# Staging the transposed weights of a stick-breaking attention in SBUF before they are split into two halves

## The chip, the cores and the metric

The kernel runs on one core of one Trainium2 chip. The core's engines work side by side and are ordered among themselves by semaphores alone: TensorE (PE; its weight loads are listed as PEld), VectorE (DVE), ScalarE (ACT), GpSimd (POOL) and SyncE (SP), which issues the DMAs here. The metric is the device time of one execution in microseconds. The kernel before takes 1668.99 us, the median of three runs (1668.65 to 1670.77).

## The reference

One layer of a streaming encoder: 1024 frames of a new stream and 32 frames of a running one, D_MODEL 1024. A combined projection feeds a retention group (4 heads) and a stick-breaking group (8 heads of 64); their outputs are projected and normalised, then come an attention into 256 memory tokens and a gated feed-forward part with a causal convolution. The change lies in the stick-breaking attention:

```python
def stick_breaking_block(q, k, v, q_pos, k_pos):
    """q (B,H,Tq,d); k,v (B,H,Tk,d). A[t,s] = beta[t,s] prod_{s<j<t}(1-beta[t,j]), s<t."""
    z = jnp.einsum('bhqd,bhkd->bhqk', q, k).astype(jnp.float32) * (SB_DH ** -0.5)
    valid = k_pos[None, :] < q_pos[:, None]
    log_fail = jnp.where(valid, jax.nn.log_sigmoid(-z), 0.0)
    after = lax.cumsum(log_fail, axis=3, reverse=True) - log_fail
    a = jnp.where(valid, jnp.exp(jax.nn.log_sigmoid(z) + after), 0.0)
    return jnp.einsum('bhqk,bhkd->bhqd', a, v.astype(jnp.float32)).astype(v.dtype)
```

All of it is fp32.

## The kernel before

Matmuls of full precision are made of faster ones: every operand is kept as two halves in the matmul type fp32r, `hi` and `lo`, with `lo = raw - hi`, and a product is `hi*hi + hi*lo + lo*hi`. The helper `split` makes the halves: ScalarE copies `raw` into `hi` with a cast (line 103), then VectorE writes `raw - hi` into `lo` (line 104). `mm` (line 119) issues a matmul.

The stages follow one another: first query/key projections and the values; a woven stage, in which the rest of the projections and the retention group run together with the stick-breaking group; the end of retention; the output projection; the memory attention; its projection; the feed-forward part.

In the woven stage the function `weave` (line 125) takes two lists of steps with costs, `main` (projections and retention tiles) and `side` (stick-breaking), and calls them in one order, so that both use up their costs at the same rate. That is the order of the code. The builder of the program then fixes the order of the instructions on each engine when it compiles, from the dependencies and its own estimates, so that neighbours in the code may change places; at run time each engine keeps its order.

A stick-breaking head works on blocks of 128 queries, i = 0 to 7, with 128*(i+1) keys:

- `score(i)` (line 421): TensorE makes scores in PSUM banks of tag "pb" (two buffers). ScalarE makes of each bank `f = sigmoid(-z/8)` (line 434) and `b = sigmoid(z/8)` (line 435), two SBUF tiles of 128x1024 with two buffers each. POOL puts 1 and 0 above the diagonal (lines 437, 439). VectorE makes of `f` the running product from the right, in place (the scan, line 441), and multiplies `b` by it, shifted by one (line 443). `b` then holds the weights, and `f` isn't read any more.
- `turn(i, g)` (line 446): TensorE transposes up to four 128x128 tiles of `b` into one PSUM bank of tag "pc" (line 457), and `split` makes the halves `ah` and `al` (tag "at", listed as `ath` and `atl`) from that bank.
- `value(i)` (line 463), for odd i: TensorE multiplies values by the halves of two blocks, into a bank of tag "pd" (listed as `pv`).

`stick_steps` (line 566) strings these together: score(i+1) comes before the turns of block i, and the values of a pair one block later still. `stick_sample` (line 483) does the same for the running stream, once for two heads.

The tag "pc" has two banks, and they are shared: retention's `turn` (lines 302 and 303, copied out by ScalarE in line 305) and `store` (line 341, copied out in line 343) take turns with the stick-breaking transposes. A bank can be written again when the readers of its last contents are done; for a stick-breaking bank these are ScalarE's cast and VectorE's subtraction. In the same way a buffer of `f` can be written again when the last reader of its former contents is done.

Other names in the trace: `acc` are the banks of projections, `rps` those of retention; `ra` and `rb` are retention's rotated queries and keys, `sg` its gate, `ss` its sum of squares, of which POOL makes the power -1/2 (lines 115 and 116) and by which ScalarE scales (line 337).

Of the kernel before, what the change touches and what calls it, by code (L numbers as in the profile page):

```python
# [18 lines left out]
NS = 32  # L19
# [47 lines left out]
def trunk(ctx: ExitStack, tc: tile.TileContext, I, O):  # L67
    nc = tc.nc
# [30 lines left out]
    def raw_tile(shape, name):  # L99
        return rawp.tile(shape, F32, name=name, tag="raw")  # L100

    def split(raw, hi, lo):
        nc.scalar.copy(hi, raw)  # L103
        nc.vector.tensor_tensor(out=lo, in0=raw, in1=hi.bitcast(F32), op=ALU.subtract)  # L104
# [13 lines left out]
    def mm(out, lhsT, rhs, start, stop):  # L118
        nc.tensor.matmul(out, lhsT, rhs, start=start, stop=stop)  # L119
# [56 lines left out]
    def tr_tile():  # L176
        return bank("pc", "tr")
# [203 lines left out]
    def z_tile():  # L381
        return bank("pb", "z")

    def pv_tile():
        return bank("pd", "pv")

    def fold_o(pv, e, w):
# [4 lines left out]
        nc.vector.tensor_tensor(out=ot[sl, :w], in0=pv[0:64, :w], in1=ot[sl, :w], op=ALU.add)  # L392
        return ot[sl, :w]

    def dup_load(raw, src):
        dma(out=raw[0:64], in_=src)
        dma(out=raw[64:128], in_=src)

    def stick_head(hd):
        m, e = hd // 2, hd % 2  # L400
        rows = slice(64 * hd, 64 * hd + 64)
        H, F, AT = {}, {}, {}

        def prepare():
            qr = raw_tile([128, NP], f"qr{hd}")
            dup_load(qr, qT_s[rows, 0:NP])
            kr = raw_tile([128, NP], f"kr{hd}")
            dup_load(kr, O["kT"][rows, 0:NP])
            vr = raw_tile([128, 8, 64], f"vr{hd}")
            dma(out=vr, in_=O["v"][0:NP, rows].rearrange("(t p) d -> p t d", p=128))  # L410
            q = sb.tile([128, NP], F32R, name="sq_", tag="sbq", bufs=2)
            nc.scalar.copy(q, qr)
            nc.vector.tensor_tensor(out=q[64:128], in0=qr[64:128], in1=q[64:128].bitcast(F32), op=ALU.subtract)
            kh = sb.tile([128, 1088], F32R, name="kh", tag="kst", bufs=3)
            kl = sb.tile([128, 1088], F32R, name="kl", tag="kst", bufs=3)
            split(kr, kh[:, :NP], kl[:, :NP])
            v = sb.tile([128, 10, 128], F32R, name="v", tag="sbv", bufs=2)
            split(vr, v[:, 0:8, 0:64], v[:, 0:8, 64:128])
            H.update(q=q, kh=kh, kl=kl, v=v)

        def score(i):
            q, kh, kl = H["q"], H["kh"], H["kl"]
            w = 128 * (i + 1)
            npc = (w + 511) // 512
            pw = max(w // npc, 256)
            f = sb.tile([128, NP], F32, name="f", tag="f", bufs=2)
            b = sb.tile([128, NP], F32, name="b", tag="b", bufs=2)
            for pc in range(npc - 1, -1, -1):
                z = z_tile()
                c0 = pc * pw  # L430
                c1 = min(c0 + pw, w)
                mm(z[:, :pw], q[:, 128 * i:128 * i + 128], kh[:, c0:c0 + pw], True, False)
                mm(z[:, :pw], q[:, 128 * i:128 * i + 128], kl[:, c0:c0 + pw], False, True)
                nc.scalar.activation(f[:, c0:c1], z[:, :c1 - c0], AF.Sigmoid, scale=-0.125)
                nc.scalar.activation(b[:, c0:c1], z[:, :c1 - c0], AF.Sigmoid, scale=0.125)
            dg = slice(128 * i, w)
            nc.gpsimd.affine_select(out=f[:, dg], in_=f[:, dg], pattern=[[-1, 128]], compare_op=ALU.is_gt,  # L437
                                    fill=1.0, base=0, channel_multiplier=1)
            nc.gpsimd.affine_select(out=b[:, dg], in_=b[:, dg], pattern=[[-1, 128]], compare_op=ALU.is_gt,
                                    fill=0.0, base=0, channel_multiplier=1)  # L440
            nc.vector.tensor_tensor_scan(out=f[:, :w][:, ::-1], data0=f[:, :w][:, ::-1], data1=f[:, :w][:, ::-1],  # L441
                                         initial=1.0, op0=ALU.mult, op1=ALU.bypass)
            nc.vector.tensor_tensor(out=b[:, :w - 1], in0=b[:, :w - 1], in1=f[:, 1:w], op=ALU.mult)
            F[i] = b

        def turn(i, g):
            half = i % 2
            if half == 0 and g == 0:
                for gg in range((i + 5) // 4):
                    AT[gg] = tuple(sb.tile([128, 4, 256], F32R, name=x, tag="at", bufs=4) for x in ("ath", "atl"))  # L450
                jz = i + 1
                for x in AT[jz // 4]:
                    nc.gpsimd.memset(x[:, jz % 4, 0:128].bitcast(F32), 0.0)
            j0, j1 = 4 * g, min(4 * g + 4, i + 1)
            tr = tr_tile()
            for j in range(j0, j1):
                nc.tensor.transpose(tr[:, 128 * (j - j0):128 * (j - j0) + 128], F[i][:, 128 * j:128 * j + 128], ident)
            src = tr[:, :128 * (j1 - j0)].rearrange("p (a b) -> p a b", b=128)
            ah, al = AT[g]
            dsl = slice(128 * half, 128 * half + 128)  # L460
            split(src, ah[:, 0:j1 - j0, dsl], al[:, 0:j1 - j0, dsl])

        def value(i):
            pv = pv_tile()
            for j in range(i + 1):
                ah, al = AT[j // 4]
                mm(pv[:, :256], H["v"][:, j], ah[:, j % 4], j == 0, False)
                mm(pv[:, :256], H["v"][:, j], al[:, j % 4], False, j == i)
            o = fold_o(pv, e, 256)
            dma_out(out=mix_s[i - 1:i + 1, 64 * e:64 * e + 64, 4 + m].rearrange("t p c -> p t c"),  # L470
                    in_=o.rearrange("p (t c) -> p t c", t=2))

        blocks = []
        for i in range(8):
            tv = [(0.7 * min(4, i + 1 - 4 * g), lambda i=i, g=g: turn(i, g)) for g in range((i + 4) // 4)]
            if i % 2:
                tv.append((0.25 * (i + 1), lambda i=i: value(i)))
            blocks.append(((0.6 * (i + 1), lambda i=i: score(i)), tv))
        return (2.0, prepare), blocks
# [3 lines left out]
    def stick_sample(m):  # L483
        H = {}
# [27 lines left out]
        def score():  # L512
            q, kh, kl = H["q"], H["kh"], H["kl"]
            f = sb.tile([128, NP], F32, name="f", tag="f", bufs=2)
            b = sb.tile([128, NP], F32, name="b", tag="b", bufs=2)
            for c0, cw in ((0, PAST), (PAST, NS)):
                z = z_tile()
                for e in range(2):
                    mm(z[:64, :cw], q[:, e], kh[:, e, c0:c0 + cw], e == 0, False)
                    mm(z[:64, :cw], q[:, e], kl[:, e, c0:c0 + cw], False, e == 1)  # L520
                nc.scalar.activation(f[:64, c0:c0 + cw], z[:64, :cw], AF.Sigmoid, scale=-0.125)
                nc.scalar.activation(b[:64, c0:c0 + cw], z[:64, :cw], AF.Sigmoid, scale=0.125)
            nc.vector.tensor_tensor(out=f[:64, PAST:NK], in0=f[:64, PAST:NK], in1=cst[:64, C_INV:C_INV + 32], op=ALU.max)
            nc.gpsimd.tensor_tensor(out=b[:64, PAST:NK], in0=b[:64, PAST:NK], in1=cst[:64, C_VAL:C_VAL + 32], op=ALU.mult)
            nc.vector.tensor_tensor_scan(out=f[:64, :NK][:, ::-1], data0=f[:64, :NK][:, ::-1], data1=f[:64, :NK][:, ::-1],
                                         initial=1.0, op0=ALU.mult, op1=ALU.bypass)
            nc.vector.tensor_tensor(out=b[:64, :NK - 1], in0=b[:64, :NK - 1], in1=f[:64, 1:NK], op=ALU.mult)
            H["b"] = b

        def turn():  # L530
            b = H["b"]
            tr = tr_tile()
            ah = sb.tile([128, 5, 64], F32R, name="ath", tag="at", bufs=4)
            al = sb.tile([128, 5, 64], F32R, name="atl", tag="at", bufs=4)
            for j in range(5):
                cw = 128 if j < 4 else NS
                nc.tensor.transpose(tr[:cw, 64 * j:64 * j + 64], b[:64, 128 * j:128 * j + cw], ident[:64, :64])
            split(tr[:, 0:256].rearrange("p (a b) -> p a b", b=64), ah[:, 0:4], al[:, 0:4])
            split(tr[:NS, 256:320], ah[:NS, 4], al[:NS, 4])
            H.update(ah=ah, al=al)  # L540

        def value():
# [14 lines left out]
        def store():  # L557
# [4 lines left out]
            dma_out(out=mixs_s[:, 4 + m], in_=ot[:, :NS])  # L562

        return (2.0, prepare), [((2.5, score), [(1.5, turn), (1.5, value), (0.3, store)])]

    def stick_steps():
# [914 lines left out]
    for t in range(4):  # L1481
        for j in range(LATE):
            i = len(STEPS) - LATE + j
# [99 lines left out]
```

## Time and profile before

| | |
|---|---|
| median of three runs | 1668.99 us |
| the profiled execution, its own time | 1672.11 us |
| its span, first to last instruction | 1670.4 us |
| granted TensorE clock, mean | 0.993 |
| HBM read, written | 163.75 MB, 42.36 MB |
| woven stage, as used here | 103 to 502 us of the span |

Lines of the profile read so. A row of instructions in order of time has its start and its duration in us, the engine, the line of the code, the operation, the tile written and the tiles read, the shape, and in brackets the engine's idle time before it with what ended that. A row of a group has the count, then the busy time in us and the mean duration in ns, then the idle time before these instructions and what ended most of it. A row of waits has the waiting engine and tile, what it waited for, and the sum in us, the number and the longest. A row of a window has the busy time of PE, PEld, DVE, ACT and POOL in it, each with its number of instructions, and the granted clock, the share of DMA and GB/s. Of the forty slices each digit is a share of busy time in tenths. The ends of matmuls are modelled.

### The profile page before, as it was taken

How to read it: one execution, taken by the hardware profiler on the slowest of the kernel's cores; microseconds unless marked ns; L12 is line 12 of the kernel's file. 1: busy time of each engine (PE TensorE's matmuls, PEld its weight loads, DVE VectorE, ACT ScalarE, POOL GpSimd, SP SyncE). 2: the span in 40 equal slices, each digit the busy share in tenths (PEclk: the TensorE clock that was granted, in tenths of full speed). 3: DMA queues.
4: the chain of work that ended last, by engine and by line, in shares of the span. 5: the costliest groups of instructions: out<-in, count | busy, mean ns of one | idle time of the engine just before them, and what ended most of it. 6: DMA issues, size and time to landing. Idle time of an engine off the chain costs nothing. (4 is left out here: it accounts for less than half of the span.)

```text
span 1670.4 us, 26878 instructions
## 1 busy us (share of the span) xinstructions
PE 1618.0 (97%) x10008; PEld 1448.5 (87%) x10008; DVE 1192.0 (71%) x1912; ACT 795.6 (48%) x1588; POOL 293.2 (18%) x616
## 2 busy tenths in 40 slices
PE   8999999989999999999999989999999999999997
PEld 8889787877777879999977879999999999888885
DVE  3147879788775575655555798777777777689968
ACT  4246556565645122543523255554555455444445
POOL 0012246453444110000001101000010000002004
PEclk9999999999999999999999989999999999999999
DMA  7244304123214443532363313232233322498942
GB/s 257 84 118 139 83 26 104 56 72 85 57 51 150 136 139 125 158 123 82 107 200 117 117 42 114 102 98 93 102 102 101 101 91 101 139 352 275 318 160 101
DMA packets 108547, 207.87 MB, mean 124 GB/s; under 512 B 23328, under 2 KB 48672, under 8 KB 108416
## 3 DMA queue, kind: packets, MB, share of 16 engines
q1 hardware_dynamic: 108416, 206.15, 38.4%
q8 instruction: 78, 1.28, 0.3%
q14 instruction: 53, 0.43, 0.1%
HBM read 163.75 MB, written 42.36 MB: 123 GB/s over the span
## 5 line engine op out<-in xcount | busy, mean ns | idle before, releaser
L1031 PE MATMUL ux<-op_s,w_t 128*128 128x266 f32 x1056 | 140.6, 288 | 1.3 <-DVE op_s L104 1.3
L1151 DVE SCALAR_TENSOR_TENSOR cv<-u,cw,cv 128x1058 f32<-128x1058 f32 x88 | 116.0, 1319 | 33.0 <-ACT cv L1149 32.9
L1031 PEld LDWEIGHTS ux<-op_s,w_t 128*128 128x128 f32 x1056 | 135.2, 191 | 2.5 <-DVE op_s L104 2.4
L1339 PE MATMUL dx<-wdo 128*128 128x512 f32 x528 | 124.3, 392 | 0.0
L1339 PEld LDWEIGHTS dx<-wdo 128*128 128x128 f32 x528 | 100.2, 190 | 21.0 <-issue 0.2
L441 DVE TENSOR_TENSOR_SCAN f<-f 128x128 f32<-128x128 f32 (+3 forms) x64 | 88.9, 1388 | 30.0 <-POOL f L437 14.0
L115 POOL TENSOR_SCALAR rs<-mv 128x1 f32<-128x1 f32 (+1 forms) x27 | 36.6, 1355 | 357.6 <-ACT junk L638 192.2
L1339 PE MATMUL dy<-wdo 128*128 128x512 f32 x396 | 93.2, 389 | 0.1
L1339 PEld LDWEIGHTS dy<-wdo 128*128 128x128 f32 x396 | 74.3, 188 | 16.0 <-DVE wdo L104 0.5
L103 ACT CAST w_t<-wup 128x512 fp32r<-128x512 f32 x88 | 54.0, 618 | 58.2 <-PE ux L1031 44.5
L104 DVE TENSOR_TENSOR w_t<-wup,w_t 128x512 fp32r<-128x512 f32 x88 | 60.4, 688 | 29.6 <-ACT w_t L103 29.6
L119 PE MATMUL acc<-wo,mh 128*128 128x512 f32 x256 | 80.3, 393 | 0.0
L1031 PE MATMUL uy<-op_s,w_t 128*128 128x266 f32 x528 | 72.0, 291 | 3.5 <-ACT op_s L103 2.5
L1031 PEld LDWEIGHTS uy<-op_s,w_t 128*128 128x128 f32 x528 | 68.8, 193 | 4.5 <-ACT op_s L103 2.9
L1031 PEld LDWEIGHTS uy<-op_x,w_w 128*128 128x128 f32 x504 | 67.8, 196 | 4.6 <-DVE u L1179 1.8
L1031 PE MATMUL uy<-op_s,w_w 128*128 128x266 f32 x528 | 70.1, 287 | 0.9 <-DVE op_s L104 0.9
L1149 ACT ACTIVATE cv<-u,cw 128x1058 f32<-128x1058 f32 x44 | 56.1, 1274 | 30.0 <-POOL u L1143 29.0
L1031 PE MATMUL uy<-op_x,w_w 128*128 128x266 f32 x504 | 68.7, 294 | 1.6 <-DVE u L1179 1.6
L1031 PE MATMUL ux<-op_x,w_t 128*128 128x266 f32 x528 | 69.3, 287 | 0.0
L1031 PE MATMUL ux<-op_x,w_w 128*128 128x266 f32 x528 | 68.8, 286 | 0.0
L1031 PEld LDWEIGHTS uy<-op_s,w_w 128*128 128x128 f32 x528 | 67.0, 189 | 1.8 <-DVE op_s L104 1.8
L1031 PEld LDWEIGHTS ux<-op_x,w_t 128*128 128x128 f32 x528 | 67.2, 190 | 0.1
(519 smaller groups left out, 4428.9 us busy)
## 6 DMA issues: line engine op xcount, KB each, us to landing
wup<-in_wup SPq DMA_DIRECT2D x44, 512.0 KB, 3.5
rdq<-hid_s SPq DMA_DIRECT2D x85, 256.0 KB, 5.3
rdq<-in_wdown SPq DMA_DIRECT2D x74, 256.0 KB, 5.4
wds<-in_wdown SPq DMA_DIRECT2D x22, 512.0 KB, 3.5
hid_s<-cv SPq DMA_DIRECT2D x22, 512.0 KB, 2.6
rwr<-in_wret SPq DMA_DIRECT2D x16, 512.0 KB, 3.6
x_s<-r SPq DMA_DIRECT2D x16, 512.0 KB, 2.6
qr<-qT_s SPq DMA_DIRECT2D x16, 256.0 KB, 4.0
```

Source lines behind the costliest of these rows:

```text
L103: nc.scalar.copy(hi, raw)
L104: nc.vector.tensor_tensor(out=lo, in0=raw, in1=hi.bitcast(F32), op=ALU.subtract)
L115: nc.gpsimd.tensor_scalar(out=out, in0=var, scalar1=eps, scalar2=None, op0=ALU.add)
L119: nc.tensor.matmul(out, lhsT, rhs, start=start, stop=stop)
L441: nc.vector.tensor_tensor_scan(out=f[:, :w][:, ::-1], data0=f[:, :w][:, ::-1], data1=f[:, :w][:, ::-1], initial=1.0, op0=ALU.mult, op1=ALU ...
L1031: nc.tensor.matmul(acc[:, j, :266], W[:, p, k], X[:, k, q, c], start=start and k == 0 and n == 0, stop=stop and k == 3 and n == 2, skip_gr ...
L1149: nc.scalar.activation(cv, u[:, 2:UW], AF.Identity, scale=cw[:, f, 2:3], bias=cw[:, f, 3:4])
L1151: nc.vector.scalar_tensor_tensor(out=cv, in0=u[:, j:UW - 2 + j], scalar=cw[:, f, j:j + 1], in1=cv, op0=ALU.mult, op1=ALU.add)
L1339: nc.tensor.matmul(acc, x[:, a, ts_], w[:, b], start=start and n == 0, stop=stop and n == 2, skip_group_check=True)
```

## The change

A new helper, `split_staged`, has ScalarE copy the PSUM bank to an SBUF tile as it is, and then calls `split` on that tile. In `turn`, the tile is the part of `f` that belongs to the same columns. So for every bank there is one ScalarE copy more; the cast and the subtraction read SBUF, and the bank's only reader is the copy. The readers of `f` are now, last of all, the subtractions. The sample's `turn` is changed likewise, with two copies for its two pieces. There are 104 splits of this kind: 96 in the heads and 8 in the samples.

```diff
+    def split_staged(tr, stage, hi, lo):
+
+        nc.scalar.copy(stage, tr)
+        split(stage, hi, lo)
+
...
-        H, F, AT = {}, {}, {}
+        H, F, FS, AT = {}, {}, {}, {}
...
             F[i] = b
+            FS[i] = f
...
             src = tr[:, :128 * (j1 - j0)].rearrange("p (a b) -> p a b", b=128)
+            stage = FS[i][:, 128 * j0:128 * j1].rearrange("p (a b) -> p a b", b=128)
             ah, al = AT[g]
             dsl = slice(128 * half, 128 * half + 128)
-            split(src, ah[:, 0:j1 - j0, dsl], al[:, 0:j1 - j0, dsl])
+            split_staged(src, stage, ah[:, 0:j1 - j0, dsl], al[:, 0:j1 - j0, dsl])
...
-            H["b"] = b
+            H.update(f=f, b=b)
...
-            split(tr[:, 0:256].rearrange("p (a b) -> p a b", b=64), ah[:, 0:4], al[:, 0:4])
-            split(tr[:NS, 256:320], ah[:NS, 4], al[:NS, 4])
+            stage = H["f"][:, 0:320]
+            split_staged(tr[:, 0:256].rearrange("p (a b) -> p a b", b=64),
+                         stage[:, 0:256].rearrange("p (a b) -> p a b", b=64), ah[:, 0:4], al[:, 0:4])
+            split_staged(tr[:NS, 256:320], stage[:NS, 256:320], ah[:NS, 4], al[:NS, 4])
```

## The prediction

> **What bounds the kernel now.** I read the page first: the shares of the engines and the forty slices.
>
> ```profile
> PE 1618.0 (97%) x10008; PEld 1448.5 (87%) x10008; DVE 1192.0 (71%) x1912; ACT 795.6 (48%) x1588; POOL 293.2 (18%) x616
> PE   8999999989999999999999989999999999999997
> DVE  3147879788775575655555798777777777689968
> ACT  4246556565645122543523255554555455444445
> ```
>
> TensorE (PE) is busy from end to end; whatever doesn't change a wait of PE changes nothing. The edited lines run where stick-breaking is woven with the projections and retention, 103 to 502 us (slices 3 to 12, where VectorE is busiest too). So next the busy times of that stretch (PE, PEld, DVE, ACT, POOL, then clock and DMA), its groups of instructions by shape, and two rows of the page for the same pair of operations with SBUF sources:
>
> ```profile
> 103.00:502.00 399.00, 380.70 (x2227) 320.17 (x2226) 319.24 (x591) 241.70 (x639) 164.39 (x340) 1.00 0.29 80
> ```
> ```profile
> L103 ACT CAST ath<-tr 128x512 fp32r<-128x512 f32 x48 | 28.2, 591 | 12.6 <-PE tr L457 11.0
> L104 DVE TENSOR_TENSOR atl<-tr,ath 128x512 fp32r<-128x512 f32 x48 | 32.7, 680 | 4.2 <-ACT ath L103 4.1
> L103 ACT CAST ath<-tr 128x384 fp32r<-128x384 f32 x16 | 7.7, 481 | 1.4 <-PE tr L457 1.2
> L103 ACT CAST ath<-tr 128x256 fp32r<-128x256 f32 x20 | 7.5, 376 | 5.0 <-PE tr L457 3.4 <-PE tr L537 1.2
> L103 ACT CAST ath<-tr 128x128 fp32r<-128x128 f32 x16 | 4.3, 269 | 3.2 <-PE tr L457 2.8
> L337 ACT ACTIVATE sg<-sg,ss 128x128 f32<-128x128 f32 x25 | 10.1, 402 | 32.2 <-POOL ss L116 29.3 <-DVE ot L392 2.1 <-DVE sg L324 0.7
> ```
> ```profile
> L103 ACT CAST w_t<-wup 128x512 fp32r<-128x512 f32 x88 | 54.0, 618 | 58.2 <-PE ux L1031 44.5
> L104 DVE TENSOR_TENSOR w_t<-wup,w_t 128x512 fp32r<-128x512 f32 x88 | 60.4, 688 | 29.6 <-ACT w_t L103 29.6
> ```
>
> PE is idle 399.0 - 380.7 = 18.3 us of this stretch, VectorE 80, ScalarE 157. The clock is full (1.00) and DMA at 0.29. The view of waits says who ends PE's idle time (us, times, longest); the rows that matter, four for PE and three for its weight loads:
>
> ```profile
> PE tr L341 <- DVE atl L104: 4.5, 5, 2.0
> PE tr L457 <- DVE atl L104: 3.3, 4, 1.4
> PE tr L302 <- DVE atl L104: 1.5, 2, 1.3
> PE tr L457 <- ACT qk L305: 1.0, 1, 1.0
> PEld tr L341 <- DVE atl L104: 6.2, 6, 2.4
> PEld tr L457 <- DVE atl L104: 4.9, 6, 1.8
> PEld pv L119 <- DVE atl L104: 2.7, 6, 0.9
> ```
>
> The first three are one thing: a transpose wants one of the two "pc" banks, and the bank still waits for VectorE's subtraction. That is 4.5 + 3.3 + 1.5 = 9.3 us in 11 waits, half of PE's idle time here. The longest of them, in order of time:
>
> ```profile
> 367.40 0.40 PE L119 MATMUL acc<-wr_0h,x 128*128 128x512 f32 x1
> 367.74 0.58 ACT L103 CAST ath<-tr 128x512 fp32r<-128x512 f32 x1
> 369.07 0.68 DVE L104 TENSOR_TENSOR atl<-tr,ath 128x512 fp32r<-128x512 f32 x1
> 369.81 0.33 PE L341 MATMUL tr<-ident,sg 128*128 128x128 f32 x1 [2.01 <-DVE atl L104]
> ```
>
> ScalarE had read the bank by 368.32, VectorE by 369.75, and PE went on 0.06 us later.
>
> **Term 1, the banks.** After the change a bank is free when ScalarE's plain copy ends, which takes the place of the cast in the queue. Here PE would wait from 367.80 to about 368.38, so 0.58 of its 2.01 us stays. Allowing some 0.4 us for each of two more such remainders, I take 9.3 - 1.3 = 8.0 us off PE. The bounds are 0 (PE only meets VectorE at the next buffer) and 6.2 + 4.9 = 11.1 us, the same stalls as the weight loads show them, whose ends aren't modelled.
>
> **Term 2, ScalarE's work.** The copies have the shapes of the casts: 48 x 591 + 16 x 481 + 20 x 376 + 16 x 269 ns = 47.9 us, and four 32-row ones of 0.2 us each. The casts now read SBUF, for which the nearest row says 618 instead of 591: 48 x 27 ns = 1.3 us. ScalarE goes from 241.7 to about 292 of 399 us, 73%; its 157 us of idle time hide that, and it costs only where someone waits for the pair. The subtractions keep their length (680 with a PSUM operand, 688 from SBUF), so VectorE's sum stays at 319. [...]
>
> **Term 3, the values' matmuls.** `value` reads the halves, and these come one copy later. That is on PE's path where PE starts within a copy of the subtraction's end. I compared the 32 groups of `value` in the heads with the last subtraction that each needs: in 12 the slack is shorter than the copy's length. The first and the last of the 12:
>
> ```profile
> 111.07 0.42 DVE L104 TENSOR_TENSOR atl<-tr,ath 128x256 fp32r<-128x256 f32 x1
> 111.72 0.28 PE L119 MATMUL pv<-atl,v 128*128 128x256 f32 x1
> 494.41 0.69 DVE L104 TENSOR_TENSOR atl<-tr,ath 128x512 fp32r<-128x512 f32 x1 [1.38 <-ACT ath L103]
> 495.16 0.39 PE L119 MATMUL pv<-atl,v 128*128 128x256 f32 x1
> ```
>
> In the first the slack is 111.72 - 111.49 = 0.23 against a copy of 0.38, in the last 0.06 against 0.59. Each lacks its copy (and 0.06 for the hand-over) less its slack; over the 12 that is 4.5 us on PE. Bounds: 0, if the copies are placed earlier than the casts were, and 12 x 0.65 = 7.8 us.
>
> **Term 4, a new wait on ScalarE.** The copy goes into `f`, the scan's tile, of which there are two. So the first sigmoid of block i+1, which writes the same buffer, must wait for the last subtraction of block i-1; until now it waited only for VectorE's product, long done. Of the 66 blocks that have such a predecessor, 37 now start that sigmoid before that subtraction ends, the first and the last of them being:
>
> ```profile
> 108.12 0.53 ACT L434 ACTIVATE f<-z 128x384 f32<-128x384 f32 x1
> 108.92 0.26 DVE L104 TENSOR_TENSOR atl<-tr,ath 128x128 fp32r<-128x128 f32 x1
> 488.26 0.55 DVE L104 TENSOR_TENSOR atl<-tr,ath 128x384 fp32r<-128x384 f32 x1
> 488.50 0.60 ACT L521 ACTIVATE f<-z 64x512 f32<-64x512 f32 x1
> ```
>
> They overlap by 1.06 and 0.31 us; all 37 sum to 52 us of ScalarE standing still, if its order stays. Behind the waiting sigmoid stand the sigmoids of `b` that free the "pb" banks, the copies of `qk` and `ro` that free "pc" banks, and retention's evacuations; POOL's selects and VectorE's scan wait for the sigmoids, PE for the `qk` copy and the banks. How much reaches PE? The nearest row is another stall at the head of ScalarE's queue: at L337 it stands 29.3 us for POOL, and PE's waits behind ScalarE's `qk` copies are 1.0 us, 3%. Doubling that, since ScalarE is now fuller, gives 6% of 52 = 3.0 us. Bounds: 0, if other work is ordered ahead of the sigmoid, and a quarter, 13 us.
>
> **The sum.** -8.0 + 4.5 + 3.0 = -0.5 us. The profiled execution takes 1672.11 us (span 1670.4), 3.1 above the median of the three runs; it would take 1671.6, and the median of 1668.99 becomes 1668.5. About 0.2%, 3.3 us, is what a measurement can tell from no change here, so this forecast is "the same".
>
> **The rivals.**
>
> Faster: the banks' gain stays whole and the costs are hidden. For it speaks that the 11 waits are real idle time of the bounding engine, and that ScalarE and VectorE have 157 and 80 us of idle time to absorb lateness; against it, that a third of the `value` groups have no slack. Terms 3 and 4 at their lower ends give -8.0, 1661.0 us, and 1657.9 with term 1 at -11.1.
>
> Slower, by term 4: ScalarE's queue is held by VectorE's backlog and so becomes the carrier of the lateness that the banks carried. Place: the first sigmoid of a block. Price: at a quarter of 52 us, -8.0 + 4.5 + 13 = +9.5, 1678.5 us. It decides once more than 13% of the 52 us reaches PE (then the sum passes +3.3). For it speaks that the waiting engine is in front of both PSUM banks and POOL's chain; against it the 3% above, and that the order of instructions on an engine isn't the code's and may move the sigmoid back.
>
> Slower, by VectorE and POOL getting into each other's way. POOL's power of `ss` takes 0.57 us alone but 1.97 beside a scan, and a subtraction with two SBUF operands took 0.69 us once and 0.85 while POOL worked:
>
> ```profile
> 364.77 1.75 DVE L441 TENSOR_TENSOR_SCAN f<-f 128x768 f32<-128x768 f32 x1
> 364.91 1.97 POOL L116 TENSOR_TENSOR ss<-ss,mhalf 128x1 f32<-128x1 f32 x1
> 376.34 0.57 POOL L116 TENSOR_TENSOR ss<-ss,mhalf 128x1 f32<-128x1 f32 x1
> 400.03 0.69 DVE L104 TENSOR_TENSOR v<-vr,v 128x512 fp32r<-128x512 f32 x1 [1.71 <-ACT v L103]
> 404.18 0.85 DVE L104 TENSOR_TENSOR v<-vr,v 128x512 fp32r<-128x512 f32 x1
> ```
>
> The 104 edited subtractions read one operand from PSUM now and both from SBUF afterwards. At 0.16 us each they would cost VectorE 16.6 us; with half of it on PE's path the sum is -0.5 + 8.3 = +7.8, 1676.8 us. Against it: VectorE is 80% busy, not full, and most POOL work is short. [...]
>
> The change doesn't free the bank: if the second bank's copy had to wait for the first bank's subtraction, since both use one tile `f`, term 1 would be nothing and the sum +7.5, 1676.5 us. Against it: POOL's select on the last columns of an `f` starts before ScalarE's sigmoid of the other columns of that `f` ends, so parts of a tile are kept apart:
>
> ```profile
> 369.73 0.29 POOL L437 TENSOR_SCALAR_AFFINE_SELECT f<-f 128x128 f32<-128x128 f32 x1 [2.85 <-ACT f L434]
> 369.96 0.57 ACT L434 ACTIVATE f<-z 128x448 f32<-128x448 f32 x1
> ```
>
> **How the numbers follow.** The same: 0.36, at 1668.5, by itself 1665.7 to 1672.3. Faster: 0.34, around 1661. Slower: 0.20 by ScalarE's wait, 0.08 by the ports, 0.02 by banks that stay held, 0.30 in all. The likeliest case holds little over a third, so the range has to reach far into both others: from 1658, the far end of the fast case (about 0.08 lies below), to 1681, beyond the three slow ones (about 0.1 lies above, where more than a quarter of the sigmoids' wait counts).
>
> **What would show it.** In the changed profile, between 103 and 502 us: the rows of PE's `tr` waiting for DVE `atl` are gone, those waiting for ScalarE's copy are below 1.5 us; 104 copies more on ScalarE, its busy time near 292 us; the wait of `pv` for `atl` rises from 2.7 towards 7 us; a new row "ACT f L434 <- DVE atl" of some tens of us; the subtraction of 512 columns within 10 ns of 680, if the ports are no matter. PE's idle time stays near 18 us. The prediction is wrong if the weave ends more than 3.3 us earlier or later with these rows as said (then a share was mis-sized), or if the order of instructions on the engines has become so different that PE's waits come from elsewhere.

## The result and the profile after

The changed kernel takes 1687.91 us (median of four runs, 1687.01 to 1689.41) against 1668.82 us of the kernel before: 19 us more, a ratio of 1.0112 with a 95% interval of 1.0100 to 1.0124. The forecast was no change, 1658 to 1681 us. It is slower than the range allowed.

In the changed code the sigmoids stand in lines 439 and 440, POOL's selects in 442 and 444, the scan in 446, the product in 448, the transposes in 463, and the new copy in 397. The page's row of engines and two of its slices:

```profile
PE 1622.9 (96%) x10008; PEld 1444.6 (86%) x10008; DVE 1196.6 (71%) x1912; ACT 838.8 (50%) x1692; POOL 303.0 (18%) x616
PE   8999998999999999999999979999999999999997
ACT  4247667676665212533541356554555445444445
```

TensorE's busy time has hardly moved (1618.0 to 1622.9); ScalarE has 104 instructions and 43 us more. The windows say where the time is. The woven stage, which took 103 to 502 us, now ends at 521.5. Busy times of PE, PEld, DVE, ACT and POOL in it and in the two stretches behind it, first after and then before:

```profile
103.00:521.50 418.50, 389.56 (x2227) 320.99 (x2226) 323.96 (x591) 284.77 (x743) 173.44 (x340) 1.00 0.28 77
521.50:970.00 448.50, 443.24 (x2595) 393.23 (x2595) 272.21 (x510) 160.92 (x345) 55.11 (x71) 1.00 0.41 131
970.00:1685.00 715.00, 693.31 (x4698) 644.09 (x4696) 576.11 (x785) 361.47 (x556) 72.81 (x195) 0.99 0.42 142
```
```profile
502.00:951.00 449.00, 443.73 (x2599) 393.78 (x2599) 272.61 (x509) 160.84 (x345) 55.57 (x71) 1.00 0.41 132
951.00:1670.00 719.00, 697.15 (x4694) 648.76 (x4692) 575.88 (x785) 361.42 (x555) 71.68 (x195) 0.98 0.42 141
```

The woven stage is 19.5 us longer, the next stretch the same, and the last one 4 us shorter at a clock of 0.99 instead of 0.98. That last difference belongs to these two executions; it is why the spans differ by 14.9 us and the medians by 19.

So 2227 matmuls take 19.5 us longer in this stage. These rows of PE's waits matter now (us, times, longest), with the weight loads' two longest, the new waits of ScalarE, and two of VectorE that have grown:

```profile
PE rps L119 <- DVE sm L312: 7.3, 10, 1.4
PE pv L119 <- DVE atl L104: 7.0, 14, 0.9
PE tr L302 <- POOL ra L297: 4.0, 3, 2.3
PE pv L119 <- ACT ath L103: 1.8, 4, 0.9
PE tr L463 <- ACT f L397: 1.3, 1, 1.3
PE tr L341 <- ACT f L397: 0.7, 1, 0.7
```
```profile
PEld rps L119 <- DVE sm L312: 12.0, 12, 1.8
PEld pv L119 <- DVE atl L104: 12.0, 17, 1.3
```
```profile
ACT f L439 <- DVE atl L104: 27.3, 32, 1.9
ACT f L528 <- DVE atl L104: 2.2, 2, 2.0
```
```profile
DVE f L446 <- POOL f L442: 28.2, 34, 1.8
DVE atl L104 <- ACT ath L103: 18.5, 21, 1.7
```

In the kernel before, the corresponding rows of 103 to 502 us were:

```profile
PE rps L119 <- DVE sm L312: 1.8, 4, 0.6
PE pv L119 <- DVE atl L104: 1.1, 2, 0.6
PE tr L302 <- POOL ra L297: 0.7, 1, 0.7
DVE f L441 <- POOL f L437: 14.0, 22, 1.6
DVE atl L104 <- ACT ath L103: 11.9, 19, 1.4
```

The edit did what it says: no transpose waits for VectorE's subtraction any more, where PE had stood 9.3 us, and the waits for the copy are 2.0 us. But PE now stands for other things: the values' matmuls (`pv`) wait for their halves, retention (`rps`) for VectorE's mask product `sm`, and retention's transposes for POOL's sum `ra`; the change touches neither `sm` nor `ra`. ScalarE's new wait at the block's first sigmoid is there, 29.5 us in 34 waits, and VectorE's scan waits for POOL's select 28.2 instead of 14.0 us. In the stage PE's idle time is 418.5 - 389.6 = 28.9 us where the prediction wanted it to stay near 18.

Since the modelled ends hide part of a stall, I counted PE's stalls another way for all kernels below: the time from one matmul's start to the next, beyond the median for that shape in the whole execution, where it is over 0.04 us, from 103 us to the last `pv` matmul. The rest of that stretch comes to 353 to 356 us in every kernel; the stalls make the difference. Beside them stands the lag: from the start of the last of a bank's transposes, plus 0.11 us, to the end of VectorE's subtraction for that bank, as a mean over the 96 banks of the heads. Stalls and lag are of the profiled execution; the medians and the ratios below are of fast executions, and three slow ones of over 4000 us (two of the kernel with the copy behind the cast, one of the kernel before) are left out.

| kernel | median us | PE's stalls us | at `tr` | at `pv` | at `rps` | lag us |
|---|---|---|---|---|---|---|
| before | 1668.8 | 43.7 | 18.7 | 4.1 | 5.2 | 2.79 |
| the change | 1687.9 | 63.0 | 15.6 | 16.8 | 13.1 | 3.95 |
| staged in the low half | 1680.8 | 57.8 | 20.9 | 10.8 | 10.3 | 3.58 |
| copy alone | 1681.1 | 55.7 | 26.2 | 5.1 | 6.3 | 3.17 |
| wait alone | 1683.4 | 55.8 | 23.1 | 6.3 | 7.6 | 3.28 |
| its control | 1670.5 | 45.5 | 18.5 | 3.8 | 6.6 | 2.80 |
| copy behind the cast | 1670.7 | 46.6 | 18.5 | 3.5 | 7.8 | 2.82 |
| high half first | 1683.3 | 57.9 | 25.8 | 5.8 | 10.8 | 3.26 |
| staged in `b` | 1684.1 | 59.0 | 20.5 | 10.3 | 12.5 | 3.70 |
| a third staged | 1674.0 | 49.8 | 19.1 | 5.5 | 8.5 | 3.33 |
| copy and wait, late bank | 1690.9 | 64.4 | 29.5 | 9.8 | 6.4 | 3.58 |
| three buffers of `f` | 1683.8 | 58.0 | 15.6 | 10.4 | 14.2 | 3.49 |
| its control | 1671.7 | 44.8 | 20.1 | 3.4 | 4.5 | 2.79 |
| no subtraction, staged | 1670.0 | 46.9 | 11.9 | 3.3 | 15.8 | - |
| no subtraction, not staged | 1664.0 | 38.5 | 9.8 | 2.5 | 11.6 | - |
| low halves last, not staged | 1667.7 | 42.0 | 16.1 | 3.2 | 6.1 | 2.72 |
| low halves last, staged | 1687.6 | 62.1 | 15.6 | 15.9 | 13.9 | 3.98 |

### The profile page after: what moved, and what is told of

It is laid out like the page before. It is cut to its first block, busy times and chain, and to the rows that moved or that the text cites. A ratio compares the mean times of both kernels' runs of the same rounds, so it can differ in the third digit from the quotient of the medians.

```text
span 1685.3 us, 26981 instructions
## 1 busy us (share of the span) xinstructions
PE 1622.9 (96%) x10008; PEld 1444.6 (86%) x10008; DVE 1196.6 (71%) x1912; ACT 838.8 (50%) x1692; POOL 303.0 (18%) x616
## 5 line engine op out<-in xcount | busy, mean ns | idle before, releaser
L446 DVE TENSOR_TENSOR_SCAN f<-f 128x128 f32<-128x128 f32 (+3 forms) x64 | 89.7, 1401 | 47.3 <-POOL f L442 28.2
L1348 PEld LDWEIGHTS dy<-wdo 128*128 128x128 f32 x396 | 74.2, 188 | 16.4 <-DVE wdo L104 1.1
L104 DVE TENSOR_TENSOR atl<-f,ath 128x512 fp32r<-128x512 f32 (+3 forms) x104 | 55.7, 546 | 19.0 <-ACT ath L103 18.5
```

The lines of the kernel that those rows point to most:

```text
L1348: nc.tensor.matmul(acc, x[:, a, ts_], w[:, b], start=start and n == 0, stop=stop and n == 2, skip_group_check=True)
```

## The experiments

The theories: (A) the wait of the first sigmoid on the last subtraction, since both use `f`, makes the 19 us; (B) the halves come later by a copy, and whoever reads them waits.

**Staged elsewhere, the copy alone, the wait alone.** The first kernel takes `f` out of the change:

```diff
-        nc.scalar.copy(stage, tr)
-        split(stage, hi, lo)
+        nc.scalar.copy(lo, tr)
+        split(lo.bitcast(F32), hi, lo)
```

> The change with another stage: the copy goes into the tile of the low halves, so f is free after VectorE's product as before the change, and everything else of the change stays (one copy more per bank, the bank free after the copy, cast and subtraction from SBUF). The copy rounds, so the low halves come out as zero and the weights lose their low part. Theory A, the first sigmoid's wait on f makes the 19 us: the time falls back to 1662 to 1672, the row of ACT f waiting for DVE atl is gone and PE's waits of rps for sm are near 5 us again. Theory B, the halves come one copy later and the values' matmuls wait for them: 1680 to 1688, and the waits of pv stay at 15 us.

Measured: 1680.8 us, ratio 1.0060 (1.0044 to 1.0076). The second kernel has the same copy, but splits the bank:

```diff
         nc.scalar.copy(lo, tr)
-        split(lo.bitcast(F32), hi, lo)
+        split(tr, hi, lo)
```

> The kernel before with the same copy ahead of each split, into the tile of the low halves, and the split still made from the PSUM bank: ScalarE's work and the later halves, without the earlier bank and without the wait on f. Theory A: little more than the banks' wait being longer by a copy, 1672 to 1678. Theory B: as slow as the change or slower, 1684 to 1694, with pv waiting 15 us or more.

Measured: 1681.1 us, 1.0064 (1.0046 to 1.0082). The third and the fourth are the kernel before with this line more, behind the split of a block's last bank; the control writes `scr`, a column of its own, in place of `FS[i][:, 0:1]`:

```diff
+            if j1 == i + 1:
+                c = al[:, 0, 128 * half:128 * half + 1].bitcast(F32)
+                nc.vector.tensor_tensor(out=FS[i][:, 0:1], in0=c, in1=c, op=ALU.add)
```

> The kernel before with the wait alone: behind the last subtraction of each block of a head VectorE adds two copies of a column of the low half into a column of f that nobody reads, so that the next block's first sigmoid in that buffer waits for the subtraction. 64 VectorE instructions more. Theory A: 10 to 19 us over its control, which writes elsewhere. Theory B: within 3 us of its control.

> Control: the same 64 small VectorE additions, written to a column of their own, so no wait on f. Both theories: 1669 to 1675, the price of 64 small instructions on an engine that is 80% busy.

Measured: 1683.4 us (1.0076, 1.0060 to 1.0092) with the wait and 1670.5 us (1.0007, 0.9998 to 1.0017) without. Both theories hold, each for a part: the wait alone costs 12.9 us over its control by the medians and 11.5 by the ratios, the copy alone 12 and 11. And the first two kernels are equal, although the first frees the bank after the copy and the second only after the subtraction. PE's waits show how. In the copy-only kernel the banks are held longer and PE stands for them:

```profile
PE tr L341 <- DVE atl L104: 6.5, 6, 2.3
PE tr L462 <- DVE atl L104: 5.1, 3, 2.5
PE tr L302 <- DVE atl L104: 4.7, 5, 2.1
PE rps L119 <- DVE sm L312: 1.9, 5, 0.7
PE pv L119 <- DVE atl L104: 1.0, 3, 0.5
```

In the staged one these three rows are gone; the stalls at `tr` are 20.9 instead of 26.2 us, but those at `pv` 10.8 instead of 5.1 and at `rps` 10.3 instead of 6.3. What the early bank gave, PE lost elsewhere. The two kernels differ in one thing more, though: the staged one's casts and subtractions read SBUF. In it retention's transposes stand for POOL's `ra`, in the copy-only one not at all:

```profile
PE tr L302 <- POOL ra L297: 6.1, 4, 2.7
```

So the equal times show what the early bank is worth together with the SBUF operands, not by itself.

In the wait-only kernel, ScalarE's row is the one that the change has too, with VectorE's new addition as the releaser:

```profile
ACT f L435 <- DVE f L466: 25.7, 22, 2.4
```

**Work or lateness.** Is the copy's cost ScalarE's 48 us of work, or that it stands ahead of the cast? The first kernel here is the kernel before with one copy behind each split, from the high half into used columns of `b` (the samples likewise); the second casts from the bank first and copies then.

```diff
             split(src, ah[:, 0:j1 - j0, dsl], al[:, 0:j1 - j0, dsl])
+            nc.scalar.copy(F[i][:, 128 * j0:128 * j1].rearrange("p (a b) -> p a b", b=128), ah[:, 0:j1 - j0, dsl].bitcast(F32))
```

> The kernel before, with a ScalarE copy of the same size behind each split that nobody waits for: the high halves are copied into the columns of b that the transposes have read, and the next writer of that buffer is ScalarE itself. ScalarE has the 48 us of work, but the cast comes first and the halves aren't later by a copy of their own. Theory B1, the halves' lateness makes the 11.7 us that the copy alone cost: 1669 to 1674, and VectorE's waits of atl for ath near 12 us as before. Theory B2, ScalarE's extra work as such, by whatever stands behind it in its queue: 1678 to 1684.

> The copy into the low halves' tile once more (low halves zero), but the cast reads the bank and comes first, then the copy, then the subtraction in place: the high halves as early as before, the low ones a copy later, the bank free after two ScalarE reads, no wait on f. B1: the subtraction stays late, so 1676 to 1682, hardly under the variant with the copy first. B2: the same 1678 to 1684. Should it be the high halves' lateness: 1669 to 1673.

Measured: 1670.7 us (1.0018, 1.0006 to 1.0031) and 1683.3 us (1.0094, 1.0077 to 1.0110). The work as such costs 3 us; the same work between the bank and the subtraction costs 12 to 15, and an early cast doesn't help when the subtraction is late. VectorE's own waits agree, in the copy-only kernel and then in the one with the copy behind:

```profile
DVE atl L104 <- ACT ath L103: 26.6, 28, 1.9
```
```profile
DVE atl L104 <- ACT ath L103: 14.6, 18, 1.6
```

VectorE stood 11.9 us for casts in the kernel before. While it stands there, retention's `sm` and `ra` stand behind: there it stood 1.05 us ahead of the subtraction at 283.65 us, and its product into `ra` followed at 284.26 and `sm` at 285.30, although the last matmuls for these two had started by 281.4.

**Where the stage lies, and how much is staged.** One kernel stages in `b` (the samples likewise); the other stages only the first bank of blocks 4 to 7 and splits all others from PSUM.

```diff
-            FS[i] = f
+            FS[i] = b
```
```diff
-            split_staged(src, stage, ah[:, 0:j1 - j0, dsl], al[:, 0:j1 - j0, dsl])
+            if i >= 4 and g == 0:
+                split_staged(src, stage, ah[:, 0:j1 - j0, dsl], al[:, 0:j1 - j0, dsl])
+            else:
+                split(src, ah[:, 0:j1 - j0, dsl], al[:, 0:j1 - j0, dsl])
```

> The change with b in place of f as the stage: the copy goes into the columns of b that the transposes have read. The whole computation. The wait moves from the block's first sigmoid to the second one, about 0.5 us later, and f is free early. If the wait at the head of ScalarE's queue costs by its length (27 us in 32 waits in the change, so some 16 us in this one): 1683 to 1686. If it costs by being there at all: 1687 to 1690.

> A third of the change: staged in f only for the first bank of blocks with two banks (32 of 104 splits), all others split from PSUM as before. The last subtraction of a block doesn't read f, so the sigmoids hardly wait. If cost goes with the number of copies and the wait on f is gone: a third of 11.5 us, 1672 to 1675. If it gains where the banks' waits are longest, behind the long scans: 1664 to 1669.

Measured: 1684.1 us (1.0099, 1.0084 to 1.0114) and 1674.0 us (1.0038, 1.0023 to 1.0053). With the stage in `b` the wait moves to the second sigmoid and is far shorter than the 29.5 us of the change:

```profile
ACT b L440 <- DVE atl L104: 8.6, 20, 1.0
```

Over the kernel before in its own series this kernel is 16 us slower, the change 19. So the time lies where a cost by length was expected, but some 70% of the wait went and 2 to 3 us came back, with intervals that overlap: that the wait costs by its length isn't shown. A third of the copies costs 6 us, in the range expected from their number, and nothing is gained behind the long scans.

**What the early bank is worth.** The change with the split made from the bank (and the wait kept by the small addition, behind a block's last bank), and the change with three buffers of `f`, in the room of a weight tile, beside the kernel before with that weight tile less:

```diff
-            split_staged(src, stage, ah[:, 0:j1 - j0, dsl], al[:, 0:j1 - j0, dsl])
+            nc.scalar.copy(stage, src)
+            split(src, ah[:, 0:j1 - j0, dsl], al[:, 0:j1 - j0, dsl])
+            if j1 == i + 1:
+                c = al[:, 0, 128 * half:128 * half + 1].bitcast(F32)
+                nc.vector.tensor_tensor(out=FS[i][:, 128 * j0:128 * j0 + 1], in0=c, in1=c, op=ALU.add)
```
```diff
-    wp = ET(tc.tile_pool(name="wp", bufs=9))
+    wp = ET(tc.tile_pool(name="wp", bufs=8))
...
-            f = sb.tile([128, NP], F32, name="f", tag="f", bufs=2)
+            f = sb.tile([128, NP], F32, name="f", tag="f", bufs=3)
```

> The change's copy into f and its wait on f (by the small VectorE addition behind the last subtraction), but cast and subtraction read the bank, so it is freed no earlier than before; in the heads alone, the samples stay as changed. The copy alone cost 11.7 us and the wait alone 12.9 us over its control. If costs add and the change's 19 us hold an early bank's gain: 24 to 28 us over the kernel before, 1692 to 1696. If the two lateness costs overlap and the early bank is worth nothing: 17 to 21 us, 1685 to 1689.

> The whole change with three buffers of f instead of two, so that no sigmoid waits for a subtraction; the room is taken from the weight tiles, 8 instead of 9. The copy waits for nothing but its transposes. If the copy's lateness costs as in the runs before: 8 to 12 us over its control. If the early bank then shows its gain of up to 8 us: 0 to 5 us over it.

> Control: the kernel before with 8 weight tiles instead of 9. 1668 to 1673.

Measured: 1690.9 us (1.0134, 1.0118 to 1.0149), 1683.8 us (1.0096, 1.0080 to 1.0113) and 1671.7 us (1.0020, 1.0010 to 1.0030). Neither expectation of the first was met: 22 us lies between 17 to 21 and 24 to 28. Beside both costs the early bank gives back at most about 3 of the 22 us, and about 1 of these can be the 64 additions, as in the control above; the intervals of the two ratios overlap. With no wait on `f` the change still costs 12 us over its control, as much as the copy-only kernel with its late banks, so there it gives back none, again together with its SBUF operands. The control itself lies 1.7 to 5 us over the kernel before.

**The chain shorter.** Subtractions left out, first in the kernel staged in the low half, then in the heads of the kernel before:

```diff
         nc.scalar.copy(lo, tr)
-        split(lo.bitcast(F32), hi, lo)
+        nc.scalar.copy(hi, lo.bitcast(F32))
```
```diff
-            split(src, ah[:, 0:j1 - j0, dsl], al[:, 0:j1 - j0, dsl])
+            nc.scalar.copy(ah[:, 0:j1 - j0, dsl], src)
...
-                mm(pv[:, :256], H["v"][:, j], al[:, j % 4], False, j == i)
+                mm(pv[:, :256], H["v"][:, j], ah[:, j % 4], False, j == i)
```

> Staged in the low halves' tile, and VectorE's 104 subtractions left out: the low half stays the rounded copy, so the weights come out doubled. VectorE has 55 us less in its queue and PE's weight products wait for ScalarE alone. If VectorE's lateness is what PE's waits in this stretch come from: 1648 to 1662, with PE's waits for sm, atl and ra below half. If ScalarE's queue is what counts: 1672 to 1682.

> The mirror image: the kernel before with one link less between transposes and values. The heads' subtractions are left out and the high halves are multiplied twice, so PE's work is the same and the weights come out doubled. Lateness theory (every link between the transposes and the next user of their results costs about 10 us, and a copy in place of the subtraction cost nothing): 1655 to 1664. If a bank or VectorE's load were the point, the link's removal frees both as well, so a time within 3 us of the kernel before would be against lateness, banks and load alike, and leave the order of instructions.

Measured: 1670.0 us (1.0010, 1.0000 to 1.0019) and 1664.0 us (0.9958, 0.9943 to 0.9972). Of 55 us of subtractions the first kernel has none left and the second 2.5 us. A copy in place of a subtraction leaves the time as it was, with 48 us more work on ScalarE; a link less gives 5 us, at the edge of what the lateness theory wanted and half of its 10 us per link. These 5 us hold everything that the second kernel relieves at once: the way to the halves, the bank, which is free after the cast, and VectorE's work. VectorE's amount of work alone therefore doesn't set the pace here; that the length of the way is a part of it agrees with both, but isn't separated from the bank.

**The values' wait relieved.** In `value`, all high halves first, then all low ones, in the kernel before and in the change:

```diff
                 mm(pv[:, :256], H["v"][:, j], ah[:, j % 4], j == 0, False)
+            for j in range(i + 1):
+                ah, al = AT[j // 4]
                 mm(pv[:, :256], H["v"][:, j], al[:, j % 4], False, j == i)
```

> The kernel before with the values' matmuls in another order: all high halves first, then all low ones, which gives the last subtraction up to 1 us more. Lateness theory with pv as the place where it is paid: 1664 to 1668, since pv's stalls were only 4 us before. Otherwise no difference, 1667 to 1671.

> The change with that order of the values' matmuls. If the values' wait for the low halves is the place where the copy's lateness is paid (16.8 us of stalls against 4.1): 1676 to 1682. If PE only meets the same lateness at its next wait, of rps for sm or of tr for ra: 1684 to 1689.

Measured: 1667.7 us (0.9988, 0.9975 to 1.0001), not told from no change, and 1687.6 us (1.0101, 1.0084 to 1.0117). In the changed kernel with this order PE's first rows are

```profile
PE rps L119 <- DVE sm L312: 8.3, 10, 1.3
PE pv L119 <- DVE atl L104: 4.6, 9, 1.0
PE tr L302 <- POOL ra L297: 4.0, 3, 2.3
PE pv L119 <- ACT ath L103: 3.5, 6, 1.2
```

The wait for the low halves falls from 7.0 to 4.6 us, that for the high ones rises from 1.8 to 3.5 and that for `sm` from 7.3 to 8.3: the sum of the three stays (16.1 and 16.4 us). The values' wait isn't the place of the cost, only one of the places where it shows.

## Why the prediction was wrong

Three of the four terms failed: the gain of term 1 came to 0 to 3 us in place of 8.0, and the later halves and the new wait of terms 3 and 4, put at 7.5 us together, cost 22 with the late bank.

**Term 1 failed, -8.0 us for the banks.** The waits named there went, and the remainder (2.0 us for the copies) was near the 1.3 us taken. But they weren't worth their length: the measured worth is 0 (equal kernels with the early and the late bank) to 3 us, together with what the SBUF operands cost. Without the bank's wait PE ran on and stood at `pv`, at `rps` and for `ra` instead. That it met the same lateness there fits the rows, but some of it may be new, from POOL's slower `ra` (see the rivals below). The kernel that frees the bank after the cast and has no subtraction in the heads at all gained 5 us, less than the 8.0 taken for the bank alone. The prediction had this as the term's lower bound, "PE only meets VectorE at the next buffer", and didn't take it for the likely value.

**Term 2 was right in size, but its price wasn't nothing.** 284.8 us of ScalarE against 292 foretold; the work as such costs 3 us where it was put at nothing. The group rows of the change:

```profile
L103 ACT CAST ath<-f 128x512 fp32r<-128x512 f32 x48 | 29.9, 626 | 0.6
L397 ACT COPY f<-tr 128x512 f32<-128x512 f32 x48 | 28.2, 590 | 4.1 <-PE tr L463 3.5
L104 DVE TENSOR_TENSOR atl<-f,ath 128x512 fp32r<-128x512 f32 x48 | 33.6, 702 | 13.1 <-ACT ath L103 12.8
L296 POOL TENSOR_TENSOR ra<-ra,rb 128x128 f32<-128x128 f32 x27 | 25.9, 959 | 50.1 <-DVE rb L288 44.6 <-DVE sm L312 5.5
```

And the last of these rows in the kernel before, 103 to 502 us:

```profile
L296 POOL TENSOR_TENSOR ra<-ra,rb 128x128 f32<-128x128 f32 x27 | 18.8, 695 | 52.1 <-DVE rb L288 42.2 <-DVE sm L312 9.1 <-PE pv L119 0.7
```

The cast takes 626 ns from SBUF where it took 591 from PSUM.

**Term 3 was mis-sized, +4.5 us for the values.** PE's stalls at `pv` rose by 12.7 us. The step that failed was to let every subtraction come later by just its copy and the hand-over, 0.65 us for 512 columns and 0.54 in the mean of the 96 banks. The mean lag rose by 1.16 us: other work gets between the copy and the cast. ScalarE at one place of the change, in order of time, with other instructions left out:

```profile
385.71 0.59 ACT L397 COPY f<-tr 128x512 f32<-128x512 f32 x1
386.19 0.55 ACT L439 ACTIVATE f<-z 128x448 f32<-128x448 f32 x1
...
387.05 0.57 ACT L439 ACTIVATE f<-z 128x448 f32<-128x448 f32 x1
...
388.26 0.60 ACT L103 CAST ath<-f 128x512 fp32r<-128x512 f32 x1
...
393.68 0.60 ACT L439 ACTIVATE f<-z 128x512 f32<-128x512 f32 x1 [1.86 <-DVE atl L104]
```

The copy ends at 386.30 and its cast starts at 388.26, behind four sigmoids and a scaling of retention. The last line is the new wait on `f`.

**Term 4 was mis-sized, +3.0 us for the sigmoid's wait.** ScalarE waits 29.5 us, not 52. That other work would be ordered ahead of the sigmoid was foreseen as a possibility; how much of the difference it makes wasn't counted. But the wait alone costs 12.9 us, some half of the 25.7 us that it lasts in its own kernel, against 6% assumed. The row that was taken as the nearest, ScalarE standing for POOL at L337, was a bad one: that little was late behind it says nothing about a stall ahead of the sigmoids, behind which POOL's select, VectorE's scan and, in VectorE's queue, all of retention wait.

The slower rival by term 4 had the right sign and place and 0.20 of the chances; at 1678.5 us it was too small, since the copy's lateness came on top (alone 12, both with a late bank 22, with an early one 19). The faster rival needed costs that were hidden, and they aren't. That the bank stays held is ruled out by the rows above. Of the rival that the prediction calls the ports, VectorE and POOL in each other's way, there is a trace: the subtraction takes 702 instead of 680 ns, 1 us over the 48 of this shape and not 0.16 us each; POOL's `ra` takes 959 ns where the same row of before had 695, though 755 with the copy alone, which keeps the PSUM operand. What lies between the two engines no run shows. The price shows on POOL rather than on VectorE: the two additions of `ra` take 1826 to 1884 ns together in all kernels whose 104 subtractions read SBUF alone (staged in `f`, in `b`, in the low half, high half first, three buffers), and 1345 to 1558 ns in the kernel before and in those with the copy alone, the wait alone, both with a late bank, and the copy behind. In the first group retention's transposes wait 4.0 to 7.3 us for `ra`, in the second 0 to 2.0. The staged third lies between in length, 1585 ns, and yet waits 5.9 us, so the wait doesn't follow from the length alone. Several of the 8 us that the early bank was to bring may have gone this way; no run takes the SBUF operands away and keeps the early bank.

What stays open: how much of the cost comes from the new order of instructions that the builder chose in each kernel, how much from POOL's longer additions, and by which paths exactly lateness turns into stalls. The order is a rival that no run holds fixed. Aligning VectorE's 659 instructions of this stage and just behind it with those of the kernel before leaves some 2 out of place in the control of the wait and 12 with the copy behind, which cost little, but 31 with the copy alone, 47 staged in the low half, 79 with the wait alone and 106 in the change. Later halves and another order came together, so the copy and the wait are shown as the causes, but not how each acts. The staged third has the lag of the wait-only kernel and half of its added stalls, so the mean lag isn't a measure by itself.

## What to carry to other kernels

A wait that heads the list of a bounding engine's waits may be worth far less than its length: here 9.3 us of such waits went, and 0 to 3 us came of it. Before buying an earlier buffer with a longer way to the data, look at who reads the data, and at what stands in the same queues behind a later reader: here a copy of up to 0.6 us between a bank and its split cost 12 us over 104 splits, while the same copy behind the split cost 3. A staging tile that is borrowed brings its owner's next writer to wait; that alone cost 13 us, and it is found in advance by listing what the next user of the tile is and where it stands now.

## What the runs showed of the hardware

VectorE's subtraction isn't faster from two SBUF operands than from PSUM and SBUF (702 and 680 ns for 128x512 in these kernels), while ScalarE's cast is slower from SBUF (626 against 591, 35 ns more). POOL's two additions of `ra` go from 1345 to 1840 ns together when VectorE's 104 subtractions take both operands from SBUF, while the subtraction itself loses 22 ns. Taking 55 us of subtractions from VectorE, 80% busy in this stage before, and giving ScalarE 48 us of copies in their place changed nothing (1670.0 us). A matmul of plain fp32 operands took TensorE 0.22 us for 128 columns, one of fp32r halves 0.12 us for 256 (from start to start, at 329.17 and 332.74 us of the kernel before).
